# Seven-product keys and key latents in a stage ahead of the attention, and a second-map scaling on ScalarE, in one encoder step on one Trainium2 core

## The chip, the core and the metric

The kernel runs on one core of a Trainium2 chip. The core has five engines, each with its own in-order queue: TensorE (PE: matrix products into PSUM; PEld is the loading of its weights), VectorE (DVE), ScalarE (ACT), GpSimd (POOL) and SyncE (SP, which here only issues DMAs). An instruction starts when it is at the head of its queue and the semaphores that it waits for have arrived; what stands behind it waits with it. The metric is the device time of one execution in microseconds (us). Before the change it was 2362.17 us, the median of three runs.

## What is computed

One layer of a streaming encoder for 592 token rows: 512 of a prompt, 16 meta tokens and 64 of a running stream. Cut to what matters here:

```python
h = rmsnorm(x, norm_attn_g)                  # 592 rows of 2048
z = h @ w_in                                 # queries, keys, values of 8 heads, latents
qd, kd, vd = ...                             # 8 heads, each 128 columns = 2 maps of 64
ckv = rmsnorm(z[..., OFF_CKV:OFF_KR], ...)   # key latents, 256 columns
s = einsum(qd, kd) * DIFF_SCALE + bias       # two maps c of every head
p = softmax(s);  p = p[:, :, 0] - lam * p[:, :, 1]
o_d = einsum(p, vd)                          # differential attention, then a norm per head
...                                          # latent attention, w_out, residual
x = x + (silu(h @ w_gate) * (h @ w_up)) @ w_down
```

All of it is wanted in float32 accuracy. A product of two float32 tiles is made of three products of rounded tiles: each operand is split into a high part (a copy to the fp32r type, by ScalarE) and a low part (source minus high part, by VectorE), and TensorE adds high x high, high x low and low x high in one PSUM bank.

## The kernel before: staging and order

**Operands.** `xh[k]` and `xl[k]` (k = 0 to 15) are the high and low parts of the input, transposed, scaled by the norm's gain, 128 features x 592 tokens each. They are made in the first stage (`transpose_x`), in which queries and keys of head 0 are also accumulated (`project_both`, banks `ps0` and `ps1`). The row factor of the norm is applied behind the product: `rb` holds it in all partitions, and a projection becomes a tile `z` by one VectorE instruction on its PSUM bank (`ps`). `ztile` has three buffers.

**Projections.** `project` makes one 128-column block of `h @ w_in` for all tokens, in two halves of 8 k. A half loads 128 x 1024 weights (`wr`), splits them (`wh` by ScalarE, L156; `wl` by VectorE, L153) and issues per k six matmuls of 296 columns (288 for queries). A block is 96 matmuls. In a trace they are `ps<-xh,wh`, `ps<-xl,wh` and `ps<-xh,wl` of L108.

**First attention.** For each head h the generator `projections` makes queries, keys and values in turn and spawns `keys` (splits into `kk`, and transposes `pna`, `pnb`, `pck` for the outputs and the cached keys), `values` (`pna`, `pnb`) and `diff_attend`. The latter goes through five blocks of queries (widths 144, 272, 400, 528 in two cuts of 264, and 192). A score piece is two matmuls into one of two banks called `sp`; VectorE reduces it with the bias (L665, a custom instruction and a short one that reads its accumulator), which frees the bank; ScalarE makes the exponentials (L669). Behind both maps of a block VectorE forms the reciprocal (L673), multiplies it (L674), scales the second map (L675) and combines both into `p` (L677). Then come transposes (`tp`, one bank), products with the values (`po`, one bank) and a norm (`pq`, and L165 to L182).

**What sets the order.** Every matmul and transpose goes through `OrderedTensorEngine`, which keeps TensorE's instructions in the order in which the program writes them. That order is made by `Streams`: it runs the generators against a planner's clock, by rank, and `take`, `give` and the numbers yielded say how long a bank or a tile is thought to be away. The projections have the last rank: they fill what the attention leaves. A list that is yielded makes a generator wait for others. So `yield [scored[h - 2]]`, `yield [nat[...]]` and `yield [att[h - 2]]` hold the projections back until older heads have come so far. The other engines' instructions stand in the order that the scheduler gives them.

**Behind it.** After head 7 come four query-latent blocks of `projections`, `second_part` (loads the stored heads, `mix_operand` splits them, L891 and L892), `latents` (transposes `pkr`, `pn`), `mix_out` (matmuls `ps<-mxh,wh`) and the latent attention (`heads`, from its matmuls `ps<-cqh,mh` on). The feed-forward part, from 850 us on, already uses seven products for a 2 x 2 block product, with operand sums by GpSimd and VectorE (L1218, L1219, L1230, L1300, matmuls L1315 and L1319); the change does not touch it.

Of the kernel before, what the change touches and what calls it, by code (L numbers as in the profile page):

```python
# [19 lines left out]
P = 128  # L20
# [78 lines left out]
class OrderedTensorEngine:  # L99
# [5 lines left out]
    def matmul(self, out, lhsT, rhs, start, stop):  # L105
        n = int(np.prod(rhs.shape[1:]))
        self.streams.now += max(n, 256) * (0.00042 if rhs.dtype == F32R else 0.00168)
        self.tc.keep_in_program_order(self.pe.matmul(out, lhsT, rhs, start=start, stop=stop))  # L108
# [7 lines left out]
def encoder_step(  # L116
# [213 lines left out]
    xspill = dp.tile([KC, P, TQ], F32, name="xspill")  # L330
# [15 lines left out]
    with ExitStack() as ph:  # L346
# [42 lines left out]
        with tc.tile_pool(name="xn", bufs=1, reuse_waits="tile") as xn:  # L389
# [83 lines left out]
            def transpose_x(kc):  # L473
# [11 lines left out]
                store(xspill[kc], xt[:, 0:TQ])  # L485
# [64 lines left out]
        pss.close()  # L550
        pst = ph.enter_context(tc.tile_pool(name="pst", bufs=1, space=PSUM, reuse_waits="tile"))
        pso = ph.enter_context(tc.tile_pool(name="pso", bufs=1, space=PSUM, reuse_waits="tile"))
        psv = pss.enter_context(tc.tile_pool(name="psv", bufs=1, space=PSUM, reuse_waits="tile"))
# [85 lines left out]
        def diff_attend(h, kk, vh, vl):  # L639
# [10 lines left out]
            for b in range(5):  # L650
# [24 lines left out]
                V.tensor_scalar(es[1][0:n, 0:W], es[1][0:n, 0:W], ls[0:n, 1:2], None, op0=ALU.mult)  # L675
# [49 lines left out]
        def projections():  # L725
# [3 lines left out]

            def queries(h, ps):  # L730
                z = ztile()
                V.scalar_tensor_tensor(hv(z, TQ), ev(ps, QH), DH ** -0.5, hv(rb, TQ),
                                       op0=ALU.mult, op1=ALU.mult)
                st.give("ps", 2.0)
                twinned[h] = st.spawn(0, twin_queries(qs[h % 2], z))

            def new_keys(h, ps):
                z = ztile()
                V.tensor_tensor(hv(z), ev(ps), hv(rb), op=ALU.mult)
                st.give("ps", 2.0)  # L740
# [3 lines left out]
            def row_factors():  # L744
                yield 4.0
                for name in ("tp", "po"):
                    yield from st.take(name)
                main, own = tbank("rm"), obank("ro")
                for j, (o, n) in enumerate(tok):
                    PE.matmul(main[:, o:o + n] if o < SEQ else own[:, 0:n], rc[0:n, j:j + 1].to_broadcast([n, P]),  # L750
                              ident[0:n, 0:n], start=True, stop=True)
                V.tensor_copy(rb[:, 0:SEQ], main)
                V.tensor_copy(rb[:, SEQ:T], own[:, 0:OWN])
                for name in ("tp", "po"):
                    st.give(name, 2.0)

            def first_rows():
# [1017 lines left out]
```

## Time and profile before

| what | value |
|---|---|
| three runs | 2360.29, 2362.17, 2363.19 us; median 2362.17 |
| profiled execution | 2363.54 us; span in the trace 2361.8 us |
| mean granted TensorE clock | 0.999 |
| first attention with its projections | about 47 to 473 us |
| mix and latent attention start | 496 us and 508 us |

A row of a group gives line, engine, operation, output and inputs, shape, count, busy us, mean ns of one, and the idle time before it with its releaser. A row of a timeline gives start, duration and what ran; `x2` merges two. A row of a stage gives its length and the busy time of PE, PEld, DVE, ACT and POOL (with counts), the granted clock (1.00 is full), DMA share and GB/s. Matmuls overlap, so two that follow each other are timed by their starts.

### The profile page before, as it was taken

The page shows a single profiled execution, that of the slowest core. Times are in us where ns is not written, and L with a number is a line of the kernel's source. Part 1 is how long each engine was busy: PE and PEld are TensorE (multiplying, and loading weights), DVE is VectorE, ACT ScalarE, POOL GpSimd, SP SyncE. Part 2 cuts the span into 40 slices and gives each one's busy share as a digit, 9 for nine tenths or more (in the row PEclk, how much of TensorE's full clock was granted, in tenths as well). Part 3 has the DMA queues.
Part 4 walks back from the last instruction along what each step waited for, and adds up shares of the span by engine and source line. Part 5 has one row for each costly group of instructions (what it writes and reads, how often), then busy time and mean ns, then how long its engine had stood idle before and what let it go on. Part 6 is the DMA issues. An engine that isn't in the chain of part 4 may idle for free. (4 is left out here: it accounts for less than half of the span.)

```text
span 2361.8 us, 43545 instructions
## 1 busy us (share of the span) xinstructions
PE 2331.1 (99%) x17336; PEld 2299.9 (97%) x17336; DVE 1862.5 (79%) x2777; ACT 1131.1 (48%) x2005; POOL 676.8 (29%) x419
## 2 busy tenths in 40 slices
PE   9999999999999999999999999999999999999998
PEld 8999999999999999999999999999999999999997
DVE  6667776676666789888898888888888888888884
ACT  6455555444454554444454454454454333333435
POOL 0000000120001446555555555554555111111110
PEclk9999999999999999999999999999999999999999
DMA  8433343263334643444444544544546884654532
GB/s 257 118 93 93 102 118 86 73 188 96 114 93 156 186 151 102 158 154 136 158 149 136 163 142 138 168 133 147 167 132 201 312 289 137 230 181 156 181 90 99
DMA packets 361626, 353.10 MB, mean 150 GB/s; under 512 B 23751, under 2 KB 318446, under 8 KB 361422
## 3 DMA queue, kind: packets, MB, share of 16 engines
q1 hardware_dynamic: 359150, 345.78, 46.4%
q0 software_dynamic: 992, 3.48, 0.5%
q8 instruction: 136, 2.23, 0.4%
q10 hardware_dynamic: 1280, 1.06, 0.2%
q14 instruction: 68, 0.56, 0.1%
HBM read 268.82 MB, written 82.34 MB: 149 GB/s over the span
## 5 line engine op out<-in xcount | busy, mean ns | idle before, releaser
L1315 PE MATMUL m<-b,wh 128*128 128x288 f32 x7280 | 1062.9, 295 | 7.8 <-ACT wh L156 3.3
L1315 PEld LDWEIGHTS m<-b,wh 128*128 128x128 f32 x7280 | 994.6, 188 | 13.0 <-ACT wh L156 9.2
L1319 PE MATMUL m<-b,wl 128*128 128x288 f32 x3640 | 581.1, 296 | 2.3 <-DVE wl L153 2.0
L1319 PEld LDWEIGHTS m<-b,wl 128*128 128x128 f32 x3640 | 515.7, 189 | 4.7 <-DVE wl L153 4.5
L153 DVE TENSOR_TENSOR wl<-raw,wh 128x1024 fp32r<-128x1024 f32 (+2 forms) x347 | 477.3, 1377 | 38.9 <-ACT wh L156 38.4
L156 ACT ACTIVATE wh<-raw 128x1024 fp32r<-128x1024 f32 (+2 forms) x347 | 313.6, 904 | 363.7 <-PE m L1315 320.2
L1300 POOL TENSOR_TENSOR ws<-raw 128x1024 f32<-128x1024 f32 (+2 forms) x85 | 173.0, 2036 | 662.4 <-DVE wl L153 339.8
L156 ACT ACTIVATE wh<-ws 128x512 fp32r<-128x512 f32 (+2 forms) x248 | 196.7, 793 | 286.5 <-PE m L1315 126.0
L153 DVE TENSOR_TENSOR wl<-ws,wh 128x512 fp32r<-128x512 f32 (+2 forms) x248 | 240.3, 969 | 7.7 <-PE m L1319 4.3
L108 PE MATMUL ps<-xh,wh 128*128 128x296 f32 (+1 forms) x992 | 222.8, 306 | 0.3 <-ACT xh L160 0.3
L108 PE MATMUL ps<-xl,wh 128*128 128x296 f32 (+1 forms) x992 | 215.2, 298 | 0.4 <-DVE xl L161 0.3
L108 PE MATMUL ps<-xh,wl 128*128 128x296 f32 (+1 forms) x960 | 207.8, 298 | 0.0
L1574 DVE TENSOR_TENSOR y<-y,m 128x288 f32<-128x288 f32 x280 | 126.2, 451 | 65.3 <-PE m L1319 64.2
L1466 DVE TENSOR_TENSOR c<-c,s 128x288 fp32r<-128x288 f32 x172 | 170.3, 990 | 0.0
L108 PEld LDWEIGHTS ps<-xh,wh 128*128 128x128 f32 x992 | 159.9, 190 | 3.3 <-issue 1.1
L108 PEld LDWEIGHTS ps<-xl,wh 128*128 128x128 f32 x992 | 160.6, 189 | 1.1 <-DVE xl L161 0.9
L108 PEld LDWEIGHTS ps<-xh,wl 128*128 128x128 f32 x960 | 155.5, 189 | 0.0
L153 DVE TENSOR_TENSOR wl<-wr,wh 128x1024 fp32r<-128x1024 f32 (+1 forms) x109 | 117.3, 1077 | 42.6 <-ACT wh L156 38.9
L1300 POOL TENSOR_TENSOR raw<-raw 128x1024 f32<-128x1024 f32 (+1 forms) x46 | 141.0, 3064 | 3.5
L156 ACT ACTIVATE wh<-wr 128x1024 fp32r<-128x1024 f32 (+1 forms) x111 | 102.0, 918 | 81.4 <-PE ps L108 57.8
L1412 DVE TENSOR_TENSOR c<-c,m 128x288 f32<-128x288 f32 x171 | 73.1, 447 | 79.1 <-PE m L1319 41.1
L1485 POOL TENSOR_TENSOR c<-c,rb 128x576 f32<-128x576 f32 x44 | 74.9, 1702 | 138.0 <-ACT c L1484 138.0
(400 smaller groups left out, 3031.9 us busy)
## 6 DMA issues: line engine op xcount, KB each, us to landing
raw<-in_ffn_w_gate SPq DMA_DIRECT2D x44, 1024.0 KB, 6.1
raw<-in_ffn_w_up SPq DMA_DIRECT2D x44, 1024.0 KB, 7.9
b<-opspill SPq DMA_DIRECT2D x147, 288.0 KB, 6.0
raw<-in_ffn_w_down SPq DMA_DIRECT2D x32, 1024.0 KB, 5.9
wr<-in_w_in SPq DMA_DIRECT2D x57, 512.0 KB, 4.1
opspill<-s SPq DMA_DIRECT2D x43, 576.0 KB, 3.1
opspill<-c SPq DMA_DIRECT2D x43, 576.0 KB, 6.7
raw<-in_ffn_w_down SPq DMA_DIRECT2D x8, 1280.0 KB, 6.1
```

Source lines behind the costliest of these rows:

```text
L108: self.tc.keep_in_program_order(self.pe.matmul(out, lhsT, rhs, start=start, stop=stop))
L153: V.tensor_tensor(lo, src, f32(hi), op=ALU.subtract)
L156: S.activation(hi, src, AF.Copy)
L1300: (G if p == 5 or p == 7 and within else V).tensor_tensor(x, y, z, op=ALU.add if p == 5 else ALU.subtract)
L1315: PE.matmul(banks[p], wh[:, k, :], x, start=first and new and k == 0 and x is hi, stop=False, skip_group_check=not new)
L1319: PE.matmul(banks[p], wl[:, k, :], hi, start=False, stop=last and k == n - 1, skip_group_check=not new)
L1412: V.tensor_tensor(c, c, banks[p], op=ALU.add)
L1466: V.tensor_tensor(src[:, k].bitcast(F32R), src[:, k], f32(hi[:, k]), op=ALU.subtract))
L1485: G.tensor_tensor(g[:, f, :], g[:, f, :], rb2, op=ALU.mult)
L1574: V.tensor_tensor(c, c, banks[p], op=ALU.add)
```

## The change

The keys of heads 1 to 6 (three pairs) and the two blocks of key latents (one pair) are taken out of `projections`. They are made ahead of the attention by `seven`, a 2 x 2 block product with seven instead of eight half-size products: the 2048 features are split into odd and even groups of 128, the 592 tokens into two halves of 296, and the two column blocks are the pair. Four of the seven products need sums of token operands; `token_sums` builds these from the stored input (`xspill`, read back and scaled by ScalarE), with GpSimd's subtractions and the usual split. Values of head 0 and queries of head 1 are also made in this stage. All results go to memory (`zspill`) and are fetched back by GpSimd's DMA queue where a head needs them (`spilled_rows`). In `diff_attend` the second map is scaled by ScalarE.

```diff
+                    t = sa.tile([P, TH], F32, name="ts", tag="ts", bufs=2)
+                    t7 = sa.tile([P, TH], F32, name="t7", tag="t7")
+                    G.tensor_tensor(t, b12, b11, op=ALU.subtract)
+                    operand7(5, t)
+                    G.tensor_tensor(t, b22, t, op=ALU.subtract)
+                    operand7(6, t)
+                    yield
+                    G.tensor_tensor(t7, b22, b12, op=ALU.subtract)
+                    operand7(7, t7)
+                    G.tensor_tensor(t, b21, t, op=ALU.subtract)
+                    operand7(4, t)
...
+            pv0 = psv.tile([P, 2, 512], F32, name="ps")
+            for n, _ in enumerate(project(pv0, w_in[:, OFF_V:OFF_V + P], xs1, ready=(both[4], both[5]))):
...
+                if n % 2:
+                    next(building)
+            scaled_rows(pv0, 7)
+            pq1 = pjt()
+            for n, _ in enumerate(project(pq1, w_in[:, P:2 * P], xs1, n=QH)):
+                if n % 2:
+                    next(building)
+            scaled_rows(pq1, 8, QUERY_SCALE)
...
+            def quarter(f, t, col):
+                pool, tag = ((sa, f"wa{t}"), (wp, "wr"))[f]
+                w = pool.tile([P, KC // 2, P], F32, name="wa", tag=tag, bufs=WR_BUFS if f else 1)
+                load(w, w_in[:, col:col + P].rearrange("(m t p) c -> t p m c", t=2, p=P)[t])
+                return w
+
+            def seven(cols, spilled):
+                a11, a12 = (quarter(0, t, cols[0]) for t in range(2))
+                a22, a21 = (quarter(1, t, cols[1]) for t in (1, 0))
+                c1, c2 = ztile("c"), ztile("c")
...
+                steps = {5: (G, w, a21, a22, ALU.add), 6: (V, w, w, a11, ALU.subtract),
+                         3: (V, a12, a12, w, ALU.subtract), 7: (V, a21, a11, a21, ALU.subtract)}
...
+                for p, name in ((1, "a"), (2, "c"), (5, "b"), (6, "a"), (3, "b"), (7, "a"), (4, "d")):
...
+                    split(wh, wl, src[p])
+                    for k in range(KC // 2):
+                        for i in range(2):
+                            PE.matmul(banks[name], wh[:, k, :], operands7[k, p][i],
+                                      start=new and k + i == 0, stop=False, skip_group_check=not new)
+                    for k in range(KC // 2):
+                        PE.matmul(banks[name], wl[:, k, :], operands7[k, p][0],
+                                  start=False, stop=k == KC // 2 - 1, skip_group_check=not new)
...
+                for c, i in zip((c1, c2), spilled):
+                    V.tensor_tensor(c, c, rb, op=ALU.mult)
+                    store(zspill[i], c)
+
+            for h in (1, 3, 5):
+                seven([OFF_K + (h + i) * P for i in range(2)], (h, h + 1))
+            seven((OFF_CKV, OFF_CKV + P), (9, 10))
...
-                V.tensor_scalar(es[1][0:n, 0:W], es[1][0:n, 0:W], ls[0:n, 1:2], None, op0=ALU.mult)
+                S.activation(es[1][0:n, 0:W], es[1][0:n, 0:W], AF.Copy, scale=ls[0:n, 1:2])
...
+            def spilled_rows(i, n=T):
+                z = ztile()
+                G.dma_start(z[:, 0:n], zspill[i, :, 0:n])
+                return z
...
             for h in range(H):
+                ps = None
+                if h > 1:
+                    ps = yield from taken()
+                    yield from project(ps, w_in[:, h * P:(h + 1) * P], xs1, n=QH)
+                    yield [scored[h - 2]]
+                queries(h, ps)
+                ps = None
+                if h == H - 1:
+                    ps = yield from taken()
+                    yield from project(ps, w_in[:, OFF_K + h * P:OFF_K + (h + 1) * P], xs1)
+                if h:
+                    yield [nat[2 * h - 1], nat[2 * h - 2]]
+                new_keys(h, ps)
```

What this does to the order shows at three places. **First**, TensorE in the scores of a middle head. Before, for head 2, `sp` is a score piece and `ps<-xh...` a projection of the next head:

```order
917 L108 MATMUL sp<-kk_2304,q10h 128x272
918 L108 MATMUL sp<-kk_2304,q10l 128x272
919 L108 MATMUL ps<-xh_88,wh 128x296 x2
920 L108 MATMUL ps<-xl_104,wh 128x296 x2
921 L108 MATMUL ps<-xh_88,wl 128x296 x2
922 L108 MATMUL sp<-kk_2305,q11h 128x272
923 L108 MATMUL sp<-kk_2305,q11l 128x272
924 L108 MATMUL ps<-xh_89,wh 128x296 x2
```

Now, for head 2, from the first piece of the block of width 400 on; ahead of it stand, just as close, a values block's last projection matmul (row 1151), `pck`, and the two pieces of width 272 (rows 1153 to 1156):

```order
1157 L108 MATMUL sp<-kk_2511,q00h 128x400
1158 L108 MATMUL sp<-kk_2511,q00l 128x400
1159 L108 MATMUL sp<-kk_2512,q01h 128x400
1160 L108 MATMUL sp<-kk_2512,q01l 128x400
1161 L108 MATMUL sp<-kk_2511,q00h 128x264
1162 L108 MATMUL sp<-kk_2511,q00l 128x264
1163 L108 MATMUL sp<-kk_2511,q00h 128x264
1164 L108 MATMUL sp<-kk_2511,q00l 128x264
1165 L108 MATMUL sp<-kk_2512,q01h 128x264
1166 L108 MATMUL sp<-kk_2512,q01l 128x264
1167 L108 MATMUL ps<-xh_86,wh 128x288 x2
1168 L108 MATMUL ps<-xl_102,wh 128x288 x2
```

Seven pieces, the last of them in rows 1165 and 1166, now stand with no projection between them. The same rows stand in heads 2 to 5, and in head 1 all pieces up to width 264 stand so.

**Second**, TensorE and GpSimd's queue where the new stage ends. TensorE has, from the last of the 672 matmuls of the four `seven` on (`m`), the transposes of head 0 before the first projection:

```order
776 L108 MATMUL m_1947<-s_7_1065,wl 128x296
777 L112 MATMUL pna<-ident,z 128x128 x4
778 L112 MATMUL pnb<-ident,z 80x128
779 L112 MATMUL pna<-ident,z 128x128 x4
780 L112 MATMUL pnb<-ident,z 80x128
781 L112 MATMUL pck<-ident,ck 128x128
782 L108 MATMUL ps<-xh_86,wh 128x296 x2
```

Before, one to six groups of six projection matmuls stood between such transposes. GpSimd's queue has at that place the fetch of head 0's keys (row 47) and, behind the bias of head 0 (row 53) and the next head's skewed bias (row 54), that of head 0's values (row 55), which the first `pna` reads; before, it had no fetch there:

```order
47 L859 DMA z<-zspill 128x592
48 L691 MEMSET pm 80x512
49 L691 MEMSET vm_2014 80x128
50 L691 MEMSET vm_2015 80x128
51 L693 MEMSET p_2019 128x256
52 L920 DMA zl_5360<-zspill 128x592
53 L769 MEMSET bias 64x64
54 L340 DMA tsk<-trow 128x656
55 L859 DMA z<-zspill 128x592
56 L859 DMA z<-zspill 128x576
57 L920 DMA zl_5362<-zspill 128x592
58 L859 DMA z<-zspill 128x592
```

**Third**, TensorE between head 7's last norm matmul (`pq`) and the mix (`mxh`, `mxl`). Before, 168 projection matmuls stand there, the last of them:

```order
2009 L108 MATMUL ps<-xh_99,wl 128x288 x2
2010 L108 MATMUL ps<-xh_100,wh 128x288 x2
2011 L108 MATMUL ps<-xl_116,wh 128x288 x2
2012 L108 MATMUL ps<-xh_100,wl 128x288 x2
2013 L108 MATMUL ps<-mxh_5825,wh 128x288 x2
```

Now 30 stand there, in rows 2155 to 2169:

```order
2154 L108 MATMUL pq<-sql,ones 128x288
2155 L108 MATMUL ps<-xh_97,wh 128x288 x2
2156 L108 MATMUL ps<-xl_113,wh 128x288 x2
2157 L108 MATMUL ps<-xh_97,wl 128x288 x2
2158 L108 MATMUL ps<-xh_98,wh 128x288 x2
```

The other projections now stand further ahead.

More of the change, by code (lines that the diff above doesn't have):

```diff
@@ L103, in __init__, with matmul @@
         self.tc, self.streams, self.pe = tc, streams, tc.nc.tensor
-    def matmul(self, out, lhsT, rhs, start, stop):
+    def matmul(self, out, lhsT, rhs, start, stop, **kw):
         n = int(np.prod(rhs.shape[1:]))
         self.streams.now += max(n, 256) * (0.00042 if rhs.dtype == F32R else 0.00168)
-        self.tc.keep_in_program_order(self.pe.matmul(out, lhsT, rhs, start=start, stop=stop))
+        self.tc.keep_in_program_order(self.pe.matmul(out, lhsT, rhs, start=start, stop=stop, **kw))
     def transpose(self, out, in_, identity):
@@ L484, in transpose_x @@
                 V.tensor_copy(xt, sp)
-                store(xspill[kc], xt[:, 0:TQ])
+                store(xspill[kc], xt)
                 if rider:
@@ L728, in taken @@
                 return pjt()
+            def spilled_rows(i, n=T):
+                z = ztile()
+                G.dma_start(z[:, 0:n], zspill[i, :, 0:n])
+                return z
             def queries(h, ps):
[L731 to L734, printed above, removed]
+                if ps:
+                    z = ztile()
+                    V.scalar_tensor_tensor(hv(z, TQ), ev(ps, QH), QUERY_SCALE, hv(rb, TQ),
+                                           op0=ALU.mult, op1=ALU.mult)
+                    st.give("ps", 2.0)
+                else:
+                    z = spilled_rows(8, TQ) if h else z_first
@@ L735, in queries @@
                 twinned[h] = st.spawn(0, twin_queries(qs[h % 2], z))
             def new_keys(h, ps):
-                z = ztile()
-                V.tensor_tensor(hv(z), ev(ps), hv(rb), op=ALU.mult)
-                st.give("ps", 2.0)
+                if ps:
+                    z = ztile()
+                    V.tensor_tensor(hv(z), ev(ps), hv(rb), op=ALU.mult)
+                    st.give("ps", 2.0)
+                else:
+                    z = spilled_rows(h)
                 kk[h % 2] = [ap.tile([P, TP], F32R, name=f"kk{c}", bufs=2) for c in range(2)]
@@ L742, in new_keys @@
                 nat[2 * h] = st.spawn(0, keys(h, z, kk[h % 2]))
[L744 to L755, printed above, removed]
@@ L772, in projections @@
                     if h >= 2:
-                        yield [scored[h - 2]]
-                    queries(h, ps)
-                    ps = yield from taken()
-                    yield from project(ps, w_in[:, OFF_K + h * P:OFF_K + (h + 1) * P], xs1)
-                    yield [nat[2 * h - 1], nat[2 * h - 2]]
-                    new_keys(h, ps)
-                    ps = yield from taken()
-                else:
-                    ps = psv.tile([P, 2, 512], F32, name="ps")
-                yield from project(ps, w_in[:, OFF_V + h * P:OFF_V + (h + 1) * P], xs1, ready=None if h else (both[4], both[5]))
@@ L785, in projections @@
[L785 to L791 removed]
+                        yield [att[h - 2]]
+                    z = ztile()
+                    V.tensor_tensor(hv(z), ev(ps), hv(rb), op=ALU.mult)
                     st.give("ps", 2.0)
                 else:
[L794 to L795 removed]
+                    z = spilled_rows(7)
@@ L805, in projections @@
                     st.spawn(2, key_latents())
+                if i in (4, 5):
+                    zs[i] = zl.tile([P, T], F32, name=f"zl{i}", tag=f"zl{i}")
+                    G.dma_start(zs[i], zspill[5 + i])
+                    continue
                 off = OFF_CQ + i * P
```

92 lines of the change are left out of this document (71 added, 21 removed).

## The prediction

> **What bounds the kernel now.** I read the page's totals first, then stages of the first attention, then single rows.
>
> ```profile
> PE 2331.1 (99%) x17336; PEld 2299.9 (97%) x17336; DVE 1862.5 (79%) x2777; ACT 1131.1 (48%) x2005; POOL 676.8 (29%) x419
> 180.00:227.50 47.50, 47.50 (x356) 46.89 (x355) 34.02 (x79) 26.12 (x55) 1.24 (x3) 1.00 0.36 102
> 199.83 0.43 PE L108 MATMUL ps<-xl,wh 128*128 128x296 f32 x2
> 200.65 0.44 PE L108 MATMUL ps<-xl,wh 128*128 128x296 f32 x2
> ```
>
> TensorE is the bound, on the whole (99%) and in the stage that the change cuts into. One head's stretch there, 47.5 us, shows it busy throughout, with VectorE at 34.0 and ScalarE at 26.1 us. Six matmuls lie between the two timeline rows (three pairs of starts), so a matmul of 296 columns costs 0.82 / 6 = 0.137 us, and one of 288 in proportion 0.133. What TensorE issues counts in full, and so does every hole in its queue. The question is whether holes appear.
>
> **Matmuls: -13.1.** Eight blocks of 96 were 768 matmuls; four `seven` with 7 products of 24 are 672. 96 x 0.137 = 13.1 us less. Nothing else on TensorE is added or dropped.
>
> **Building token sums: +5 (1 to 12).**
>
> ```profile
> 46.82 3.04 SPq L137 DMA_DIRECT2D wr<-in_w_in  x2
> 47.21 0.43 PE L108 MATMUL ps<-xh,wh 128*128 128x296 f32 x2
> L1230 POOL TENSOR_TENSOR bs<-xg 128x288 f32<-128x288 f32 x16 | 13.1, 820 | 16.0 <-ACT xg L1363 16.0
> L1230 POOL TENSOR_TENSOR bs<-xg,bs 128x288 f32<-128x288 f32 x16 | 15.7, 982 | 33.9 <-ACT xg L1363 25.0 <-DVE b L1219 8.9
> L1219 DVE TENSOR_TENSOR b<-bs,b 128x288 fp32r<-128x288 f32 x32 | 18.8, 589 | 3.5 <-ACT b L1218 3.5
> L1363 ACT ACTIVATE xg<-x,gT 128x576 f32<-128x576 f32 x16 | 12.5, 778 | 13.7 <-DVE x L1361 12.3 <-DMA x<-x1spill 1.4
> L1300 POOL TENSOR_TENSOR ws<-raw 128x1024 f32<-128x1024 f32 x43 | 113.6, 2643 | 254.4 <-DVE wl L153 246.4 <-DVE c L1424 8.0
> ```
>
> The feed-forward part does the same on nearly equal tiles. TensorE begins head 0's values at 47.2; 96 of these matmuls, 96 of 288 columns for queries and 48 of products 1 and 2 end at 79.7; product 5 then asks for its eighth operand at 81.6. SP issues the first read-back behind `wr` at 49.9. With some 3 us of landing and two scalings of 0.78, GpSimd starts near 54.7. Product 5's last operand is its 29th subtraction or so, at 0.82 to 0.98, with one weight sum of 2.64 between: 28.8 us, 83.5, and a split behind it, 84.5. That is 3 us late if GpSimd never waits. But products 5, 6 and 4 of a group share one tile in place, so each subtraction waits for VectorE's split of the one before, with two tiles in turn. I take 5; 1 if the chains interleave well, 12 if half of the chains lie bare.
>
> **Between two `seven`: +4 (0 to 10).**
>
> ```profile
> wr<-in_w_in SPq DMA_DIRECT2D x57, 512.0 KB, 4.1
> L156 ACT ACTIVATE wh<-wr 128x1024 fp32r<-128x1024 f32 x75 | 79.4, 1059 | 61.3 <-PE ps L108 57.0 <-issue 1.8 <-ACT q01h L620 0.9
> L153 DVE TENSOR_TENSOR wl<-wr,wh 128x1024 fp32r<-128x1024 f32 x6 | 7.3, 1224 | 3.6 <-ACT wh L156 3.5
> L1300 DVE TENSOR_TENSOR ws<-ws,raw 128x1024 f32<-128x1024 f32 x43 | 54.2, 1259 | 1.4
> ```
>
> A product takes 24 x 0.137 = 3.3 us. The quarter `a22` is read last, by product 4, whose split starts when product 3 gives its `wh` back: 16.4, and 1.06 and 1.22 later the next `a22` may load. Landing 4.1 (two loads, some 5), GpSimd's sum 2.64, VectorE's 7th-product difference 1.26, which stands ahead of product 2's `wl` in VectorE's queue, and that `wl` 1.22: about 29. TensorE wants it at 8 x 3.28 + 16 x 0.137 = 28.4. So about 1 us at each of three borders, a little more for issue; ends 0 and 3 us each.
>
> **Start of the attention: +13 (9 to 18).**
>
> ```profile
> 49.96 0.53 SPq L137 DMA_DIRECT2D ck<-in_cache_diff_k  x1
> 56.29 0.14 POOL L642 MEMSET bias<- 64x64 f32 x1 [11.20 <-DMA bias<-tsk]
> 56.38 0.56 POOL L339 DMA_DIRECT2D tsk<-trow  x1
> cos<-c_cos POOLq DMA_DIRECT2D x1, 296.0 KB, 3.1
> ```
>
> Before, this chain ran beside head 0's values block. Now head 0's `ck`, `cv` and bias wait for the last product, whose operands lay where their tiles lie. From `ck` to the memset behind the bias it was 6.3 us; then the skew's issue 0.6, the values' fetch 0.6 and 3.1: 10.6. GpSimd's queue is in order, so the fetch cannot pass the memset. Behind it TensorE does `pna`, `pnb`, `pna`, `pnb`, `pck` in one bank, each waiting for a copy out: some 4.6. TensorE's own share is 2: 13 us of hole. A bias that lands in less, and copies that overlap, give 9; a stuck queue 18.
>
> **Scores without projections: +32 (20 to 40), and +9.5 (5 to 13) for head 1.**
>
> ```profile
> L790 DVE TENSOR_TENSOR z<-ps,rb 128x592 f32<-128x592 f32 x8 | 6.2, 775 | 0.2
> L665 DVE CUSTOM_DVE_ANT_0 e<-sp,bias 128x400 f32<-128x400 f32 x16 | 8.7, 570 | 0.0
> L665 DVE CUSTOM_DVE_ANT_0 e<-sp,bias 128x272 f32<-128x272 f32 x16 | 6.5, 436 | 1.1 <-PE sp L108 1.1
> L665 DVE CUSTOM_DVE_ANT_0 e<-sp,bias 128x264 f32<-128x264 f32 x16 | 6.8, 428 | 1.3 <-PE sp L108 0.6
> L665 DVE DVE_READ_ACCUMULATOR2_ANT nm<- 128x1 f32 x80 | 6.7, 84 | 0.0
> L612 DVE TENSOR_TENSOR kk<-pck,kk 64x128 fp32r<-64x128 f32 x2 | 0.6, 289 | 0.1
> L178 DVE TENSOR_TENSOR sq<-sq,r 128x576 f32<-128x576 f32 x1 | 0.8, 751 | 0.0
> L182 DVE SCALAR_TENSOR_TENSOR r<-sq,r 128x576 f32<-128x576 f32 x1 | 0.8, 755 | 0.0
> L673 DVE RECIPROCAL ls<-ls 128x2 f32<-128x2 f32 x4 | 0.7, 164 | 2.0 <-ACT e L669 2.0
> L677 DVE SCALAR_TENSOR_TENSOR p<-e,ls 128x272 f32<-128x272 f32 x1 | 0.5, 501 | 0.0
> L669 ACT ACTIVATE e<-e,nm 128x272 f32<-128x272 f32 x16 | 8.3, 518 | 13.5 <-DVE nm L665 13.5
> L675 DVE TENSOR_SCALAR e<-e,ls x40: 295/362/496, 85.7 to 446.7; 128x144 f32<-128x144 f32 x8, 128x272 f32<-128x272 f32 x8, 128x400 f32<-128x400 f32 x8, 128x528 f32<-128x528 f32 x8
> ```
>
> Seven pieces share two banks, and each later piece waits for VectorE to free one. VectorE's queue from the end of the values block to the freeing of the last bank wanted is: `z` 0.78, two pieces of 272 at 0.52, `kk` 0.29, a piece of 400 at 0.65, `kk` 0.29, L178 0.75, reciprocal 0.16, a `wl` 1.22, the multiplication 0.16, then a wait for ScalarE's scaling, `p` 0.50, the norm's next step 0.76, the other 400 at 0.65, L182 0.76, a cut of 264 at 0.51. The scaling, which was 0.36 on VectorE, I price like the exponential of that width, 0.52. Sum 9.0 us, 9.3 until TensorE is back. Its own work in it is 2.1 (4272 columns). A hole of 7.2, and 0.8 at the eighth piece: 8 us, four times. With VectorE's other work out of the way, seven reductions alone (4 us) would leave 2; I take 5 a head as lower end, 10 as upper. Head 1 starts its scores behind head 0's last value products, also bare; the same counting gives 15 us with 5.4 of TensorE work.
>
> **Cover lost behind head 7: +12.5 (8 to 18).**
>
> ```profile
> 473.19 0.29 PE L108 MATMUL pq<-sql,ones 128*128 128x288 f32 x1
> 508.07 0.54 PE L108 MATMUL ps<-cqh,mh 128*128 128x288 f32 x2
> 480.00:520.00 40.00, 37.10 (x265) 35.04 (x263) 32.97 (x47) 22.03 (x40) 8.98 (x9) 1.00 0.68 198
> ```
>
> From the last `pq` to the heads of the latent attention it took 34.9 us, with some 3 of idling. 138 projection matmuls, 18.3 us, now lie ahead, so TensorE has 13.5 left there. The chain (norm, stored heads read back, splits, rotation, transposes) stays. Without the projections' splits in the queues I make it 29 us: 15.5 idle, 12.5 more than before; 24.5 and 35 are the ends.
>
> **Clock: +12 (0 to 17).**
>
> ```profile
> 5.00:10.00 5.00, 3.00 (x17) 2.01 (x16) 1.57 (x3) 1.94 (x3) 0.00 (x0) 1.00 1.04 303
> 10.00:15.00 5.00, 5.00 (x26) 4.98 (x27) 3.31 (x5) 1.99 (x4) 0.00 (x0) 0.66 1.15 287
> ```
>
> Once in this trace TensorE idles for long (2 of 5 us), and the clock granted in the next 5 us is 0.66: 1.7 us lost. Seven such holes (start, head 1, four heads, tail) at 1.7 are 12. The trace bears it out for that one hole only, so the lower end is 0. The Trainium skill, "TensorE: Matmul & The Clock Gate", Part 1, says that the gate halves the clock after a whole idle window of about 3.4 us. By that rule a stretch in which scores keep trickling may cost nothing, and the sum would be some 6 us lower; no run so far shows which.
>
> **Sum.** -13.1 + 5 + 4 + 13 + 32 + 9.5 + 12.5 + 12 = +74.9 on the profiled execution's 2363.5, so 2438.4. That execution is 1.4 above the median of the runs: **2437 us**. All lower ends together give 2392, all upper ends 2477. VectorE loses 40 scalings, 14.5 us, and ScalarE gains some 21; neither is a bound of a stage, so this counts only in the queue above. Stores to and fetches from memory add about 12 MB over 120 us, beside 102 GB/s in the row quoted first: hidden, except at the start.
>
> **Rivals.** (1) *TensorE stays the bound everywhere*: the planner's holes close, because VectorE, which has 34 us of work per 47.5, reaches each reduction as soon as its piece is written. Then only the matmuls count: 2349. The first stage row, with no idle at all, speaks for it; against it, the bare scores would have to end within about 1 us of TensorE's own work, while the queue's rows add up to 7 more. It decides where all holes together stay under 13.1 us. (2) *Short holes*: the scores wait for little more than the reductions (2 to 5 us a head) and the clock stays up: 2400 to 2418. For it: rows of other instructions in the queue may be done early. (3) *The new stage is bound by VectorE and GpSimd*, whose `ws` and `wl` rows in the feed-forward part are longer when both run: building 12, borders 10, the attention as forecast: 2450, with the upper ends elsewhere 2477. That fewer matmuls are not issued is excluded by the counts of the order.
>
> **Chances.** Forecast (2418 to 2456) 55%; rival 2 (2392 to 2418) 22%; rival 3 and longer holes (2456 to 2485) 18%; rival 1 3%, something between it and rival 2 2%. The range for 8 in 10 is 2400 to 2470. A measurement of this kernel tells 0.2% (4.7 us) from no change; faster by more 3%, within 2%, slower by more 95%.
>
> **What would show it.** In the trace of the changed kernel: 96 fewer TensorE matmuls; an idle gap of 9 to 18 us between the last `m` of L108 and the first `ps` row; in heads 2 to 5 a stretch of 9 to 10 us with fourteen `sp` rows and idle put down to VectorE; a gap behind head 7; granted clock under 1.00 in those slices. If the page shows TensorE at 99% there, the forecast is wrong at the scores; if the gaps are there and the clock stays 1.00, only the last term falls.

## The result: slower by 4.7%, and the profile after

| | before | changed |
|---|---|---|
| median of four runs | 2361.7 us | 2472.5 us (2472.3 to 2473.3) |
| ratio to before | 1 | 1.047, 95% interval 1.0452 to 1.0488 |
| span of the profiled execution | 2361.8 us | 2471.5 us |
| mean granted TensorE clock | 0.999 | 0.976 |

The forecast was 2437 us with a range to 2470. The sign and the kind of loss were right: holes in TensorE's queue, with a lower clock behind them. The loss of 111 us was half as large again as the forecast 75.

The page of the changed kernel, its totals and two rows of the 40 slices (one slice is 62 us; a 9 is 90% or more):

```profile
PE 2357.4 (95%) x17240; PEld 2313.2 (94%) x17240; DVE 1906.1 (77%) x2809; ACT 1192.4 (48%) x2121; POOL 721.3 (29%) x466
...
PE   9797889997999999999999999999999999999998
...
PEclk9898889998999999999999999999999999999999
```

TensorE issues 96 instructions fewer, as counted, and is busy for 26 us longer. It idles most in slices 2, 4 to 6 and 10, between the new stage and the chain behind head 7, and its clock sinks in the same slices. The same stretch, cut where the work changes (length, then busy time of PE, PEld, DVE, ACT and POOL, granted clock, DMA share, GB/s):

```profile
47.00:75.00 28.00, 27.19 (x203) 26.72 (x201) 17.60 (x24) 14.99 (x26) 13.27 (x14) 1.00 0.77 229
75.00:107.00 32.00, 15.45 (x89) 14.97 (x89) 26.60 (x30) 18.26 (x34) 20.20 (x20) 0.79 0.37 107
107.00:187.00 80.00, 80.00 (x586) 79.83 (x584) 50.07 (x55) 31.48 (x39) 7.17 (x3) 1.00 0.39 114
187.00:212.00 25.00, 9.64 (x44) 8.21 (x43) 14.68 (x26) 12.82 (x28) 4.98 (x12) 0.59 0.62 188
212.00:285.00 73.00, 63.89 (x402) 58.98 (x401) 43.62 (x119) 38.66 (x90) 2.14 (x6) 0.84 0.30 83
...
312.00:460.00 148.00, 125.81 (x854) 120.11 (x853) 101.50 (x258) 89.79 (x202) 5.16 (x14) 0.91 0.34 94
460.00:582.00 122.00, 118.13 (x869) 116.01 (x868) 73.08 (x164) 61.83 (x126) 14.60 (x16) 0.99 0.28 79
582.00:620.00 38.00, 22.86 (x111) 19.22 (x110) 27.81 (x42) 18.00 (x36) 6.26 (x5) 0.69 0.64 179
```

Length minus PE's busy time is the idle time of a stage: the building of the token sums (75 to 107), none in the rest of the seven-product stage (107 to 187), the start of the attention (187 to 212), head 1 (to 285), heads 2 to 5 (312 to 460), heads 6 and 7 (to 582) and what follows head 7 (to 620). What ended the longest waits, from the view of TensorE's waits (total us, times, longest):

```profile
PE sp L108 <- DVE nm L792: 25.0, 19, 4.4
PE m L108 <- ACT wh L156: 17.2, 3, 12.5
PE pna L112 <- DMA z<-zspill: 10.9, 1, 10.9
PE ps L108 <- ACT mxh L1007: 6.4, 1, 6.4
...
PE pn L112 <- DVE kr L1017: 3.8, 1, 3.8
```

`sp` is a score piece that waits for VectorE's reduction to free a bank; `m` a seven-product matmul that waits for a split of its weights; `pna` the first transpose of head 0's values; `mxh` and `kr` belong to the chain behind head 7. The lost clock is read from rows of 2.5 us: PE's busy time times (1 − clock) is what the matmuls there took longer than at full clock. This is called half-clock time below. For head 2's hole:

```profile
315.00:317.50 2.50, 0.00 (x0) 0.00 (x0) 1.88 (x4) 1.63 (x5) 0.00 (x0) 0.73 0.00 0
317.50:320.00 2.50, 0.63 (x2) 0.50 (x2) 2.43 (x6) 0.65 (x3) 0.00 (x0) 0.50 0.71 209
320.00:322.50 2.50, 2.29 (x10) 2.11 (x10) 2.15 (x8) 1.28 (x4) 0.00 (x0) 0.50 0.21 79
322.50:325.00 2.50, 2.50 (x20) 2.50 (x20) 1.28 (x7) 0.97 (x4) 0.00 (x0) 0.90 0.18 52
```

That is 0.63 x 0.5 + 2.29 x 0.5 + 2.50 x 0.10 = 1.7 us. Summed in this way from 60 to 640 us it is 34.7 us. So the account of the trace is:

| place | forecast, with 1.7 us of clock for each hole | idle | half clock |
|---|---|---|---|
| 96 matmuls fewer | −13.1 | −13.1 | |
| building the token sums | 5 | 0.8 + 16.6 | 3.2 |
| borders between `seven`s | 4 | 0 | 0 |
| start of the attention | 13 + 1.7 | 15.4 | 4.0 |
| head 1 | 9.5 + 1.7 | 9.1 | 9.1 |
| heads 2 to 5 | 32 + 6.8 | 22.2 | 9.8 |
| heads 6 and 7 | 0 | 3.9 | 1.7 |
| behind head 7 | 12.5 + 1.7 | 15.1, of which about 3 were there before | 7.0 |
| sum | 74.9 | some 67 | some 35 |

That is 102 of 109.7 us. Another 4 lie in the feed-forward part, which the change doesn't touch: from its first scaling (`xg`) to its last sum (`y`) it took 1567.5 us instead of 1563.2. In the profiles of the experiments it took 1562 to 1569, so this much is variation from run to run. The rest isn't attributed.

### The profile page after: what moved, and what is told of

The parts are those of the page before. It is cut to its first block, busy times and chain, and to the rows that moved or that the text cites. A ratio compares the mean times of both kernels' runs of the same rounds, so it can differ in the third digit from the quotient of the medians.

```text
span 2471.5 us, 43713 instructions
## 1 busy us (share of the span) xinstructions
PE 2357.4 (95%) x17240; PEld 2313.2 (94%) x17240; DVE 1906.1 (77%) x2809; ACT 1192.4 (48%) x2121; POOL 721.3 (29%) x466
## 5 line engine op out<-in xcount | busy, mean ns | idle before, releaser
L1431 PEld LDWEIGHTS m<-b,wh 128*128 128x128 f32 x7280 | 994.1, 188 | 16.6 <-ACT wh L156 13.1
L153 DVE TENSOR_TENSOR wl<-raw,wh 128x1024 fp32r<-128x1024 f32 (+2 forms) x347 | 475.1, 1370 | 38.8 <-ACT wh L156 38.3
L1416 POOL TENSOR_TENSOR ws<-raw 128x1024 f32<-128x1024 f32 (+2 forms) x85 | 174.1, 2048 | 664.0 <-DVE wl L153 303.8
L108 PE MATMUL ps<-xh,wh 128*128 128x288 f32 (+1 forms) x736 | 169.6, 313 | 0.4 <-ACT xh L160 0.3
L108 PE MATMUL ps<-xl,wh 128*128 128x288 f32 (+1 forms) x736 | 164.2, 305 | 0.7 <-DVE xl L161 0.7
L108 PE MATMUL ps<-xh,wl 128*128 128x288 f32 (+1 forms) x704 | 155.5, 303 | 0.1
L1528 DVE TENSOR_TENSOR c<-c,m 128x288 f32<-128x288 f32 x171 | 73.1, 447 | 78.9 <-PE m L1435 42.9
L108 PEld LDWEIGHTS ps<-xh,wh 128*128 128x128 f32 x736 | 123.2, 197 | 3.3 <-issue 1.1
L108 PEld LDWEIGHTS ps<-xl,wh 128*128 128x128 f32 x736 | 123.7, 196 | 1.4 <-DVE xl L161 1.1
L153 DVE TENSOR_TENSOR wl<-wr,wh 128x1024 fp32r<-128x1024 f32 (+1 forms) x93 | 96.5, 1038 | 31.2 <-ACT wh L156 27.3
L108 PEld LDWEIGHTS ps<-xh,wl 128*128 128x128 f32 x704 | 117.4, 195 | 0.4 <-DVE wl L153 0.4
L156 ACT ACTIVATE wh<-wr 128x1024 fp32r<-128x1024 f32 (+1 forms) x95 | 84.9, 893 | 67.7 <-PE ps L108 42.1
L1601 POOL TENSOR_TENSOR c<-c,rb 128x576 f32<-128x576 f32 x44 | 74.9, 1703 | 138.0 <-ACT c L1600 138.0
```

The lines of the kernel that those rows point to most:

```text
L153: V.tensor_tensor(lo, src, f32(hi), op=ALU.subtract)
L156: S.activation(hi, src, AF.Copy)
L1416: (G if p == 5 or p == 7 and within else V).tensor_tensor(x, y, z, op=ALU.add if p == 5 else ALU.subtract)
L1431: PE.matmul(banks[p], wh[:, k, :], x, start=first and new and k == 0 and x is hi, stop=False, skip_group_check=not new)
L1528: V.tensor_tensor(c, c, banks[p], op=ALU.add)
L1601: G.tensor_tensor(g[:, f, :], g[:, f, :], rb2, op=ALU.mult)
```

## Experiments

Kernels that were run on one chip share their runs of the kernel before; across chips the ratio to it is compared. In the table, "against the changed kernel" is the ratio less 1.0468 (the changed kernel run again), times 2363 us. Each interval is about ±4 us, so differences below some 6 us are not clear by themselves.

| run | median | ratio | against the changed kernel |
|---|---|---|---|
| after_again | 2473.9 | 1.0468 (1.0449 to 1.0488) | 0 |
| warm_steps | 2470.1 | 1.0447 (1.0432 to 1.0463) | −5 |
| warm_all | 2468.6 | 1.0438 (1.0421 to 1.0456) | −7 |
| no_sums | 2447.7 | 1.0355 (1.0337 to 1.0372) | −27 |
| vec_sums | 2469.1 | 1.0450 (1.0436 to 1.0465) | −4 |
| no_readback | 2470.0 | 1.0455 (1.0439 to 1.0470) | −3 |
| vec_no_readback | 2463.2 | 1.0425 (1.0408 to 1.0442) | −10 |
| xr1 | 2487.5 | 1.0523 (1.0506 to 1.0541) | +13 |
| early | 2473.8 | 1.0460 (1.0445 to 1.0476) | −2 |
| latents_tail | 2449.7 | 1.0358 (1.0341 to 1.0375) | −26 |
| two_pairs | 2457.3 | 1.0405 (1.0387 to 1.0422) | −15 |
| release | 2510.6 | 1.0614 (1.0599 to 1.0630) | +35 |
| dve_scale | 2466.7 | 1.0430 (1.0414 to 1.0445) | −9 |
| scale_alone | 2362.8 | 0.9998 (0.9989 to 1.0007) | (edit of the kernel before) |
| best | 2440.9 | 1.0332 (1.0317 to 1.0346) | −32 |

Each trace is one execution of these. Where its first `xg` starts tells what was gained ahead of the feed-forward part: at 858.8 us in the changed kernel, 861.6 in warm_steps, 855.1 in warm_all, 842.0 in latents_tail, 852.9 in dve_scale, 848.2 in vec_no_readback and 825.1 in best.

> The changed kernel once more, unedited, so that the runs of this chip can be compared with it. No theory differs: 2472 to 2477 us beside a kernel before of 2362 to 2365.

### Does the half clock cost what its rows say?

```diff
+        def warm(bank, n):
+            for _ in range(n):
+                behind(nc.tensor.matmul(bank[:, 0:QH], ones_r, xh[0][:, 0:QH], start=True, stop=True))
```

In `diff_attend`, ahead of the second cut of the widest block, `warm(obank("warm"), n)` with n by head.

> The changed kernel, with extra matmuls that nobody reads (128x288, 0.133 us each) in the hole of 4.4 us ahead of the fourth block's second cut: 29 for head 2 (3.9 us), 18 for head 3 (2.4 us), 9 for head 4 (1.2 us), none for head 5. Theory A (behind a hole TensorE's halved clock costs time of its own, and the prediction sized it too small): heads 2 and 3 run on at clock 1.00 and save about 1.7 to 2.8 us each, head 4 shows how much idle time it takes, head 5 stays as it was; in all 4 to 7 us less than the changed kernel. Rival B (VectorE sets the pace behind the hole, so the clock costs nothing there): clock 1.00 in heads 2 and 3, but the time within 1.5 us of the changed kernel's.

Heads 2 to 5 of warm_steps: the row behind the hole (what is left of it in brackets), and a row of 5 us behind it for each head.

```profile
321.52 0.39 PE L108 MATMUL sp<-kk,q00h 128*128 128x264 f32 x1 [0.57 <-DVE nm L798]
363.63 0.39 PE L108 MATMUL sp<-kk,q10h 128*128 128x264 f32 x1 [2.03 <-DVE nm L798]
407.20 0.59 PE L108 MATMUL sp<-kk,q00h 128*128 128x264 f32 x1 [3.21 <-DVE nm L798]
451.46 0.59 PE L108 MATMUL sp<-kk,q10h 128*128 128x264 f32 x1 [4.40 <-DVE nm L798]
```

```profile
322.50:327.50 5.00, 4.96 (x37) 4.75 (x38) 3.94 (x15) 2.57 (x6) 0.00 (x0) 1.00 0.28 79
365.00:370.00 5.00, 5.00 (x29) 4.80 (x28) 2.45 (x10) 2.18 (x5) 0.00 (x0) 0.66 0.31 100
407.50:412.50 5.00, 4.79 (x20) 4.48 (x20) 3.52 (x13) 2.56 (x7) 0.00 (x0) 0.50 0.25 87
452.50:457.50 5.00, 5.00 (x21) 5.00 (x22) 3.10 (x12) 2.41 (x6) 0.00 (x0) 0.50 0.24 79
```

Head 2 keeps its clock, and head 3's first piece of 400 columns follows head 2's after 42.1 us instead of 43.0: 0.9 us less, not the 1.7 to 2.8 of A. Head 3, with only 2.0 us left of its hole, loses its clock, which A did not expect, and saves nothing. The wait itself stays where it was: VectorE sets its end. The 5 us of the table are within the noise, and this trace reaches `xg` no earlier than the changed kernel's.

> The changed kernel with extra matmuls that nobody reads in the holes of the building (85 and 24), of the start of the attention (75), of head 1's scores (26) and of the scores of heads 2 to 5 (29 each). The waits stay; only the clock should change. Theory A: 20 to 26 us less than the changed kernel, which is the half-clock time of these places in its trace (3.2 + 4.0 + 9.1 + 9.8). Rival B: within 3 us of the changed kernel.

In the building `warm` writes into the bank that the next product starts, and at the start into the bank of the first transposes. The stages of warm_all that answer to those above:

```profile
75.00:107.00 32.00, 28.19 (x205) 27.48 (x206) 27.11 (x29) 18.72 (x34) 20.07 (x19) 1.00 0.38 106
187.00:212.00 25.00, 16.46 (x101) 15.01 (x100) 14.22 (x25) 12.58 (x27) 5.00 (x12) 0.80 0.60 179
212.00:285.00 73.00, 64.36 (x431) 60.43 (x430) 41.92 (x114) 37.60 (x87) 1.61 (x5) 0.91 0.30 81
312.00:460.00 148.00, 139.91 (x1020) 133.59 (x1019) 105.32 (x267) 93.61 (x210) 5.30 (x15) 1.00 0.36 97
```

The clock rose where it was meant to, at the start and in head 1 only in part: of 4.0 and 9.1 us of half-clock time 3.0 and 5.3 are left, so that some 18 of the 26 us are gone. The time fell by about 7 us, of which the trace shows 4 ahead of `xg`: far less than the 20 to 26 of A, and not clear of the 3 of B. The trace shows where the gain lies. From head 2's first piece of 400 columns to head 5's it took 126.2 us instead of 130.6:

```profile
314.02 0.45 PE L108 MATMUL sp<-kk,q00h 128*128 128x400 f32 x1 [0.62 <-DVE nm L805]
...
440.22 0.45 PE L108 MATMUL sp<-kk,q10h 128*128 128x400 f32 x1 [0.61 <-DVE nm L805]
```

(In the changed kernel these rows stand at 313.14 and 443.73.) There projections follow the hole, and TensorE's own speed counts. In the building the other engines set the end, and faster matmuls only wait longer: the last seven-product matmuls come 1.0 us earlier (184.84 instead of 185.82), though 3.2 us of half-clock time are gone. At the start, head 0's first piece of 400 columns comes 1.3 us later (221.17 instead of 219.84), behind a copy by VectorE that is late.

Runs without fillers say the same of heads 2 to 5. TensorE idles there for 5.5 us a head in each of them, and the distance from one head to the next is 42.9 us where 1.6 us of half-clock time lie in it (no_readback), 43.0 with 1.7 and 43.6 with 2.4 (the changed kernel), and 44.4 with 3.2 (early). Between these heads the half clock costs nearly what its rows say.

### What sets the building?

```diff
 for m in range(KC // 2):
+    for p in range(4, 8):
+        operands7[m, p] = operands7[m, 1]
+    for _ in range(3):
+        yield
+    continue
```

> The changed kernel without the token sums: the read-back, the scalings, GpSimd's 32 subtractions and their splits are left out, and products 4 to 7 take product 1's token operands. Theory A (the building fills the queues of GpSimd, ScalarE and VectorE for 42 us, and the weights of products 2 and 5 wait behind it): both holes (12.5 and 3.8 us) and their half clock go, 18 to 23 us less. Rival B (the weight quarters and their differences are late by themselves): a hole of 5 us or more stays ahead of product 2 or 5, less than 10 us gained.

27 us: the building's holes and their half clock (20.6 us) are gone, and the first transpose at the start of the attention waits 4.5 us instead of 10.9, probably since no operand tiles lie any more where the attention's tiles do. Rows of no_sums, a stage and a matmul:

```profile
75.00:165.00 90.00, 90.00 (x664) 90.00 (x663) 57.55 (x62) 36.38 (x48) 7.76 (x4) 1.00 0.39 113
```

```profile
169.82 0.69 PE L112 MATMUL pna<-ident,z 128*128 128x128 f32 x4 [4.51 <-DMA z<-zspill]
```

Why the building is long was open. The subtractions of the changed kernel between 57 and 100 us (count, busy us, mean ns, idle before and its releaser):

```profile
L579 POOL TENSOR_TENSOR ts<-xr 128x296 f32<-128x296 f32 x8 | 8.5, 1066 | 14.3 <-ACT xr L568 14.3
L581 POOL TENSOR_TENSOR ts<-xr,ts 128x296 f32<-128x296 f32 x8 | 7.9, 982 | 5.0 <-ACT xr L568 2.8 <-DVE s L153 2.2
L586 POOL TENSOR_TENSOR ts<-xr,ts 128x296 f32<-128x296 f32 x8 | 7.7, 960 | 2.3 <-DVE s L153 2.3
L584 POOL TENSOR_TENSOR t<-xr 128x296 f32<-128x296 f32 x8 | 7.6, 956 | 0.0
```

32 subtractions of about 1.0 us and 8.6 us of waits (21.6 less the 13.0 ahead of the first), with one weight sum of 2.6: 42 us for eight groups. Part of this is that both engines take longer beside each other: a subtraction takes 0.82 us where VectorE rests (57.74 in the trace) and up to 1.80 beside VectorE (67.08), and a split of this size takes VectorE 0.45 us where GpSimd rests (65.77) and up to 1.09 beside GpSimd's subtractions (77.45). Four runs change the limits of the building.

```diff
-                    G.tensor_tensor(t, b22, t, op=ALU.subtract)
+                    V.tensor_tensor(t, b22, t, op=ALU.subtract)
...
-                    G.tensor_tensor(t, b21, t, op=ALU.subtract)
+                    V.tensor_tensor(t, b21, t, op=ALU.subtract)
```

> The changed kernel with two of the four subtractions of every group of token sums (those for products 6 and 4) made by VectorE instead of GpSimd. Theory A (the rate of GpSimd's subtractions, 32 in 42 us, sets the end of the building): GpSimd's share halves, product 5 starts 6 to 14 us earlier, 6 to 14 us less in all. Rival B (ScalarE's queue or the read-back sets the end: splits and scalings stand in it one behind the other): the building ends within 3 us of where it did, and the time is within 3 us of the changed kernel's.

```diff
-                    rows_ = [sa.tile([P, T], F32, name="xr", tag=f"xr{t}", bufs=2) for t in range(2)]
-                    for t, r in enumerate(rows_):
-                        load(r, xspill[2 * m + t])
-                        S.activation(r, r, AF.Copy, scale=gA[:, 2 * m + t:2 * m + t + 1])
+                    rows_ = [f32(xh[2 * m + t]) for t in range(2)]
```

> The changed kernel whose token sums are built from the high parts that lie on the chip instead of the stored input: the read-back from memory and its scalings by ScalarE are left out (the sums then lack the low parts of their inputs). GpSimd's 32 subtractions stay. Theory A (each group goes through read-back, scaling, subtraction and split, and two sets of buffers let only two groups be under way: that sets 5.2 us a group): the groups come at 4.2 us or less, the first 8 us earlier, the holes of the building go but for 4 us, 14 to 20 us less in all. Rival B (GpSimd's subtractions and the splits behind them set 5.2 us a group): the rate stays, only the earlier start counts, 6 to 11 us less.

xr1 is the edit `bufs=1` in the first of these lines; vec_no_readback is both edits above together.

> The changed kernel with one set of buffers for the read-back instead of two. Theory A (the number of groups under way sets the rate): the groups come one behind the other, at 8 to 10 us each instead of 5.2, 22 to 40 us more in all. Rival B (GpSimd's rate): 8 us more or less than that.

> The last two edits together: token sums from the high parts on the chip (no read-back, no scalings; the sums lack the low parts), and two of the four subtractions of a group by VectorE. Taking away GpSimd's share alone gave some 4 us, taking away the read-back alone some 3. Theory A (two limits at nearly the same rate, GpSimd's subtractions at 1.0 us each and the read-back with two groups under way: either alone leaves the other): together 12 to 20 us less than the changed kernel, the building ends by 80 us in the trace. Rival B (a third limit, the splits on ScalarE and VectorE with the weights' splits behind them): 8 us less or below that.

The stretch of the building in the changed kernel, in vec_sums, in no_readback and in vec_no_readback (same columns):

```profile
57.70:99.70 42.00, 24.91 (x171) 23.95 (x169) 33.15 (x38) 27.42 (x51) 33.47 (x33) 0.88 0.52 150
```

```profile
58.00:100.00 42.00, 32.61 (x210) 31.34 (x209) 38.91 (x58) 29.50 (x55) 18.21 (x17) 0.87 0.60 175
```

```profile
51.00:92.00 41.00, 30.27 (x191) 28.96 (x191) 34.77 (x43) 16.91 (x34) 33.96 (x30) 0.85 0.27 76
```

```profile
50.00:97.00 47.00, 40.41 (x278) 39.87 (x277) 42.26 (x66) 20.81 (x40) 17.00 (x14) 0.89 0.34 95
```

No single limit holds. With half of GpSimd's share gone (33.5 to 18.2 us busy) GpSimd waits for the read-back and VectorE is at 38.9 of 42. Without the read-back GpSimd is busy for 34.0 of 41 us, so its rate stays, as B had it; TensorE's holes up to product 5 fall from 17.2 to 10.7 us, new ones in the projections among them, and the time by 3, less than B's 6 to 11 (the noise is 6). With both gone VectorE is busy for 42.3 of 47 us, and the gain is 10: between A and B. One set of read-back buffers costs 13, less than A's 22 and more than B's 8. In the changed kernel GpSimd and VectorE are busy for 33 of these 42 us each and ScalarE for 27, and each waits for the others in turn; one limit that explains the 42 us was not found.

### Start of the attention

```diff
-                    z = spilled_rows(7)
+                    z = zx.tile([P, T], F32, name="z0", tag="zl6")
+                    G.dma_start(z, zspill[7])
```

> The changed kernel with head 0's values fetched into a tile of their own, which is free at that time, instead of one of the three buffers that the last two stores of the stage still hold. GpSimd then issues the fetch ahead of the bias's memset. Theory A (the fetch is what TensorE waits for, and it waits for a buffer and behind the memset): the hole of 10.9 us ahead of the first transpose shrinks to 4 to 7, 4 to 8 us less in all. Rival B (what follows, the keys' splits and the bias, is as late, so the wait only moves): within 2 us of the changed kernel.

GpSimd issues the fetch at 190.29 instead of 194.85, and the first transpose starts 6.4 us behind it instead of 3.2. GpSimd's queue and then TensorE in early:

```profile
190.29 0.55 POOL L908 DMA_DIRECT2D z<-zspill  x1
...
191.82 0.14 POOL L769 MEMSET bias<- 64x64 f32 x1 [0.44 <-DMA bias<-tsk]
```

```profile
196.73 1.09 PE L112 MATMUL pna<-ident,z 128*128 128x128 f32 x4 [9.14 <-DMA z<-zspill]
...
203.60 0.44 PE L112 MATMUL pnb<-ident,z 128*80 128x128 f32 x1 [3.06 <-ACT na L725]
```

The hole shrinks by 1.8 us and a later wait grows from 1.6 to 3.1. Up to head 0's first piece of 400 columns 2.3 us are gained (it starts 31.7 us behind the last seven-product matmuls instead of 34.0), and heads 2 to 5 lose them again: they follow each other at 44.4 us, with 3.2 us of half-clock time in each. So the time is as B had it, and B's reason covers only a part. The chain from `ck` over the memset to the fetch, which the prediction followed, is not the only one of that length.

### Cover

latents_tail drops the fourth `seven` and lets `projections` make both blocks of key latents again (the four lines `if i in (4, 5)` go); two_pairs does the same for the keys of heads 5 and 6 (`for h in (1, 3)`, `if h > 4`). release moves one hold of the planner:

```diff
-                        yield [att[h - 2]]
+                        yield [multiplied[h - 2]]
```

> The changed kernel with the two blocks of key latents made by eight half products in the projections behind head 7 again, as before the change; the keys of heads 1 to 6 stay with seven products. Matmuls: 24 more (3.2 us). Theory A (behind head 7 the cover is missing): the 15 us of holes and 7 us of half clock there go mostly, 12 to 20 us less in all. Rival B (the chain behind head 7 is set by VectorE and ScalarE, which the returned blocks load with splits as well): no gain or up to 5 us.

> The changed kernel with the keys of heads 5 and 6 made by eight half products among the projections again; heads 1 to 4 and the key latents stay with seven. Matmuls: 24 more (3.2 us). In the recorded order the bare scores of heads 4 and 5 are filled again, those of heads 1 to 3 are not. Theory A (a pair's cover is worth more than its matmuls: 8 us for each head whose scores lie bare): 12 to 16 us less. Rival B (the holes come from the order at the start of the attention, not from missing cover): no gain, or 3 us more for the matmuls.

> The changed kernel with one hold of the planner moved forward: a head's values leave their bank when the products with the values of the head two before are done, not when its norm is done too. In the recorded order the next queries then reach into the scores, and the run of bare score pieces shrinks from 7 to 6, but the last products with the values are now bare. Theory A (the stage lacks work to fill with: 192 projection matmuls a head are less than one head's chain takes): the hole only moves, within 8 us of the changed kernel. Rival B (that hold alone bares the scores): heads 1 to 5 lose their holes and half clock, 25 to 45 us less.

latents_tail gains 26 us, more than A had, with 24 matmuls (3.2 us) more. The profiled execution is the slowest of its four and gains 19, within A's 12 to 20. Its stretch behind head 7 (this row) is at full clock, with 3.6 us of idle time in 44:

```profile
560.00:604.00 44.00, 40.38 (x290) 38.37 (x289) 36.73 (x50) 24.05 (x42) 11.35 (x12) 1.00 0.63 182
```

two_pairs gains 15, also with 3.2 us more of matmuls: 9 us for each head that gets its cover back. release loses 35 us. The holes moved to the products with the values and multiplied; in release, for one head, the longest of them:

```profile
359.83 0.52 PE L112 MATMUL tp<-ident,p 128*128 128x128 f32 x3 [3.06 <-DVE kk L739]
```

From head 2 to head 3 TensorE idles for 7.8 us instead of 5.5, and 7.6 us are half-clock time instead of 1.7. So moving this hold didn't help: at neither of the two places do 192 projection matmuls a head cover its chain, and used earlier they are missed later. That it would cost as much as 35, most of it by the clock, was expected by neither.

### The scaling by ScalarE

> The changed kernel with the second map's exponentials scaled by VectorE again, as before the change. Theory A (VectorE's queue waits for ScalarE's scaling ahead of the reduction that frees a bank): 0.8 us less in each bare score stretch of heads 1 to 5, and in all 2 to 6 us less. Rival B (VectorE is the engine that TensorE waits for, and 40 x 0.36 us back on it lengthen the stretches): 3 to 8 us more.

> The kernel before with one edit of the change alone: the second map's exponentials are scaled by ScalarE. TensorE is busy throughout there, so theory A (the scaling's place matters only where the scores lie bare): within 2.5 us of the kernel before. Rival B (the trip to ScalarE lengthens each head's chain also under cover): 3 to 8 us more.

By itself the edit costs nothing: 0.9998. In the changed kernel it costs some 9 us (±6), of which the trace shows 6 ahead of `xg`. It shows little of this in the bare scores of heads 2 to 5, where the last wait is 4.18 us instead of 4.40 and the heads follow each other no faster. Behind head 6 the waits ahead of `pnb` and `tp` are 0.69 and 0.65 us instead of 1.57 and 1.09, the clock stays up, and head 7's first piece of 400 columns follows head 6's after 41.9 us instead of 45.1. Another 2.5 us lie ahead of head 2's. So an edit that costs nothing under cover costs time once the stage has holes.

### The helpful parts together

> The changed kernel with what helped by itself: key latents behind head 7 again, two of four token-sum subtractions on VectorE, the second map scaled by VectorE, and 29 extra matmuls in the hole of the scores of heads 2 to 5. Theory A (the parts lie at different places and add up: 24, some 8, 7 and 5): 2425 to 2440 us. Rival B (they share one cause, as in the building and the start of the attention): 2440 to 2455. No theory makes it faster than the kernel before.

2440.9 us: faster than the changed kernel by 32 us, at the border between A and B, and slower than the kernel before by 3.3%. No edit of the changed kernel was as fast as the kernel before.

## Why the prediction missed

**Right**: the 96 matmuls; that the start, the bare scores and the stretch behind head 7 open holes; that VectorE's reductions end the waits of the scores. Heads 2 to 5 took 32.0 us with their clock (38.8 forecast), and undoing two of them gave 9 us each (9.7 forecast). Their idle time alone was forecast too large, 32 us for 22.2, and so were the borders, 4 us for none (80.00 of 80.00 us busy). It is by luck that these two hide 14 us of what the other terms lacked.

**The step that failed first is the building, +5 (1 to 12)**: 17.4 us of idle time in the trace, 20.6 with its half-clock time, and 27 when it is left out, of which 6 belong to the start of the attention. The working took one engine, GpSimd, at 0.82 to 0.98 us a subtraction, starting at 54.7. The first came at 57.7, a subtraction took 1.0 us, and 8.6 us of waits for read-back, scaling and splits lay between. And the hole opened where no sum was needed: product 2 wants only tiles that are there, but the split of its weights stood in ScalarE's queue behind operand splits that wait for GpSimd (the group with 12.5 us of wait for `wh`). I had put the wait at product 5.

**The second is the stretch behind head 7, 12.5 (8 to 18)**: from the last `pq` to the latent heads it was to shrink from 34.9 to 29 us. In the changed kernel it is 34.9 again (578.16 to 613.07, the first row), so all 18.3 us of moved projections were lost:

```profile
578.16:613.07 34.91, 19.77 (x104) 16.13 (x102) 28.39 (x42) 17.36 (x34) 6.26 (x5) 0.71 0.62 171
564.80:599.77 34.97, 18.40 (x104) 15.30 (x102) 28.21 (x42) 17.35 (x34) 6.29 (x5) 0.75 0.61 172
```

The idle time in it is what the working had, 15.1 us (15.5). What the working lacked is 5.3 us of half-clock time in this stretch, and 1 us of matmuls. Whether the half clock itself made it longer stays open: in two_pairs (the second row) it is 3.9 us, the idle time 16.6, and the stretch is as long. The 3 us of idling before, which the working subtracts, were read from a window that reaches beyond the stretch; within it they were 1.65. Heads 6 and 7 had holes of their own (3.9 + 1.7), at the transposes of head 7's values, where none were forecast. latents_tail gave back 26.

**The clock, +12 (0 to 17)**, is the third, and by the rows the largest: it came out as 35 us of half-clock time, three times the forecast. What it costs by itself differs from place to place. In heads 2 to 5 it is nearly all of the 9.8 us there; in the building it is 1.0 of 3.2 (warm_all), since other engines set the end. At the start, in head 1 and behind head 7 it isn't settled, because fillers didn't keep up the clock there or weren't put there. What failed for certain is the unit, one hole at 1.7 us: in head 1 and behind head 7 work trickles, and the clock stays at 0.50 for 24 us in each, in one spell (258.2 to 282.0) and in two (585.8 to 596.1 and 602.9 to 616.5). The sentence that a stretch of trickling work may cost nothing doesn't hold there. Each spell begins in a hole of 3 us or more, and rows with work in them stay at 0.50:

```profile
267.50:270.00 2.50, 2.31 (x7) 1.74 (x7) 1.76 (x7) 1.19 (x4) 0.00 (x0) 0.50 0.00 0
607.50:610.00 2.50, 1.52 (x6) 0.65 (x4) 0.85 (x2) 1.65 (x4) 0.00 (x0) 0.50 0.33 84
```

**Rival 3**, a new stage bound by VectorE and GpSimd (2450 to 2477), has the result in its range, though not by its terms: the building was 20 rather than its 12 and the borders 0 rather than 10. Its 18% were too few.

## What to carry to other kernels

Work that fills another stage's waits costs little where it stands. Taken out and done elsewhere it costs its full time there, and the waits lie bare: a `seven` saved 3.3 us of matmuls, and each of the two heads that lost their fill by it lost about 9. Before moving fill work, count for each stretch what its chain takes without it, and what is left to cover it. A preparation that runs through three engines and a read-back is priced by its chain and by what else stands in each queue, not by the slowest engine's row.

## Not expected of the hardware

The clock fell to one half after a hole of only 2.0 us (head 3 of warm_steps). The rows of 0.5 us show it fall when matmuls had been running again for 2 us:

```profile
361.50:362.00 0.50, 0.10 (x1) 0.00 (x0) 0.21 (x1) 0.26 (x1) 0.00 (x0) 1.00 0.00 0
362.00:362.50 0.50, 0.00 (x0) 0.00 (x0) 0.50 (x2) 0.00 (x0) 0.00 (x0) 1.00 0.48 91
...
365.50:366.00 0.50, 0.50 (x5) 0.30 (x3) 0.37 (x2) 0.45 (x1) 0.00 (x0) 0.88 0.00 0
366.00:366.50 0.50, 0.50 (x2) 0.50 (x3) 0.28 (x1) 0.50 (x2) 0.00 (x0) 0.50 0.50 194
...
369.00:369.50 0.50, 0.50 (x5) 0.50 (x5) 0.00 (x0) 0.00 (x0) 0.00 (x0) 0.71 0.78 127
```

The spell lasted 3.4 us, and the one in head 2 of the changed kernel 6.8: one and two times the window of some 3.4 us that the Trainium skill gives ("TensorE: Matmul & The Clock Gate", Part 1). That it falls after an idle window, as the same part has it, the trace bears out only if half busy counts as idle: the 3.4 us ahead of the fall had some 1.7 us of matmuls. The three long spells named above, 23.9, 10.2 and 13.6 us, are seven, three and four times 3.4. The same hole of 4.4 us costs a different time in each head: heads 2 to 5 of the changed kernel follow each other at 43.0, 43.6 and 44.0 us, and with fillers at 42.1 each time. Free-running windows, as the same part describes them, would explain this; no run here tests it.
